# Conditioning chunks of the output stage issued by GpSimd instead of SyncE in a hybrid decoder block

## The chip, the cores and the metric

The kernel runs on one core of a Trainium2 chip. The metric is the device time of one execution in microseconds (us). The other times in this document come from profiled executions: one execution that the hardware profiler recorded, with times from the start of its span.

## What is computed

One decoder layer for two groups of requests, a prompt of 256 tokens and 8 samples of 4 tokens, which share all weights. Each layer turns a conditioning vector `c` into six vectors (shift, scale and gate, twice), mixes with a pooling mixer and a Mamba-2 mixer, projects back with `w_out`, adds the gated result, and ends with a gated feed-forward part.

```python
def block(x, c, st_pool, st_conv, st_ssm, st_ffn, pos0, lp):
    mod = silu(c) @ lp['w_ada'] + lp['b_ada']
    sh1, sc1, g1, sh2, sc2, g2 = split(mod, 6)
    h = rmsnorm(x, lp['norm1']) * (1 + sc1) + sh1
    u_pool, z, xbc, dt_raw = split(h @ lp['w_in'])
    pool_out, new_pool = pool_mixer(u_pool, st_pool, ...)
    ssd_out, new_conv, new_ssm = ssd_mixer(z, xbc, dt_raw, st_conv, st_ssm, ...)
    mix = concatenate([pool_out, ssd_out]) @ lp['w_out']
    x = x + g1 * mix
    h2 = rmsnorm(x, lp['norm2']) * (1 + sc2) + sh2
    ffn_out, new_ffn = conv_ffn(h2, st_ffn, ...)
    x = x + g2 * ffn_out
```

The width is 2048 and all values are 32-bit floats. The six vectors are called parts 0 to 5 here. Part 2 is `g1`, part 3 is `sh2`, part 4 is `sc2`, part 5 is `g2`.

## The kernel before

**Tiling.** The 2048 channels are 16 tiles of 128 partitions (`KT` = 16). The prompt's 256 columns and the samples' 32 are worked on side by side, 288 columns in a matmul. Each product in 32-bit precision is made of three matmuls for every 128x128 block of weights (`mm3`): high half of the weight by high half of the operand (L312), high by low (L313), low by high (L314). The high half of a weight chunk is a cast on ScalarE (`whi_...`, L298), the low half a subtraction on VectorE (`wlo_...`, L300).

**Weights.** All weights come from one array in chunks of at most 128x1024 floats, 512 KB. `load` takes a slot of a ring of buffers and issues the transfer (L279) on SyncE's queue (SP). Two rings matter here: `raw` for weights that are split, such as `raw_out_m_h` (half h of output block m), and `rawa` for conditioning chunks, such as `raw_adap_4_k_h` (part 4, channel tile k, half h), which are multiplied as they are (L414). In the output stage the ring `rawa` has thirteen slots in three pools: 4, and 4 and 5 that are added as room comes free.

**Conditioning.** `ada_visits` loads the chunks of a part ahead and then, in visits, multiplies them (`whole`). For part 4 a visit covers four channel tiles, so 8 chunks and 32 matmuls of 512 columns; there are four visits in the output stage, behind the blocks m=3, 6, 9 and 12.

**Output stage.** It makes 16 blocks m of `x + g1 * mix`. For each m `out_units` runs 16 channel tiles: 12 into the accumulator `mm_out`, 4 into `mm_outp`, 48 matmuls in all. VectorE then scales `mm_out` by the norm (`oz`, L1179), adds it and `mm_outp` to the prompt's columns of `x` (L1169) and makes the samples' product `rs` (L1172), which GpSimd adds to `x` (L1175). ScalarE squares the new `x` (`sqa`, L1185) and GpSimd sums the squares (`rt`, L1187 and L1189). Loads of `x` (L1213) are issued by SP. `mixl` (L1121) is the low half of the operand of this stage, made by VectorE ahead of it.

**GpSimd's other work here.** It writes the state `o_pool` (L1115), loads `stf` (the feed-forward state, L1280) and prepares `gb` buffers for the feed-forward part (a memset at L1291, a copy out of `stf` at L1292).

**What sets the order.** Each engine executes its instructions in one fixed order. The order isn't that of the source: a scheduler places every instruction, transfers included, by when it reckons its inputs and its buffer slot to be there. Instructions marked `keep_in_program_order` keep theirs. A transfer's completion is counted on one of 8 lanes for SP and ScalarE together and 8 for GpSimd, taken in turn. A transfer is issued only when the one that had the same lane before it has landed.

Of the kernel before, what the change touches and what calls it, by code (L numbers as in the profile page):

```python
# [18 lines left out]
P = 128  # L19
# [35 lines left out]
AK, AO = 2, 4  # L55
# [28 lines left out]
def _xbc_chunks(bi):  # L84
    (k0, gk), (a, b) = BLOCKS[bi]
    mper = RAWC // (gk * P)
    cuts = [a, *([4, 8] if bi == 0 else []), *range(a + (12 if bi == 0 else mper), b, mper), b]
    return [(list(range(k0, k0 + gk)), list(range(m, n))) for m, n in zip(cuts, cuts[1:])]
# [35 lines left out]
def _halves(nk):  # L124
    return [(0, 8), (8, nk - 8)]
# [41 lines left out]
def kernel(ctx: ExitStack, tc, ins, outs):  # L167
    nc = tc.nc
    S = _STREAM
    wflat = ins["wflat"]  # L170
# [102 lines left out]

    wp = [None]

    def load(key, ring="raw"):
        off, cols = S.items[key]
        t = wp[0].tile([P, RAWC], F32, tag=ring, name="raw_" + "_".join(map(str, key)))
        nc.sync.dma_start(t[:, :cols], wflat[off:off + P * cols].rearrange("(p n) -> p n", p=P))  # L279
        return t  # L280

    queue = deque(_need_order())
    ahead = {}
    nloads = [0]

    def top_up():

        while queue and nloads[0] - min((n for n, _ in ahead.values()), default=nloads[0]) < RAW0 + RAW1 + RAWA:
            key = queue.popleft()
            ahead[key] = (nloads[0], load(key))  # L290
            nloads[0] += 1
# [4 lines left out]
    def split_steps(raw, a, n, name):  # L296
        hi = wp[0].tile([P, RAWC], F32R, tag="whi", name="whi_" + name)
        yield nc.scalar.copy(hi[:, :n], raw[:, a:a + n])  # L298
        lo = wp[0].tile([P, RAWC], F32R, tag="wlo", name="wlo_" + name)
        yield hi, lo, nc.vector.tensor_tensor(lo[:, :n], raw[:, a:a + n], hi[:, :n].bitcast(F32), ALU.subtract)  # L300
# [17 lines left out]
    def project_units(key, nk, opnd=None, order=None):  # L318

        name = "_".join(map(str, key))  # L320
        ps = pm.tile([P, 512], F32, tag="mm", name="mm_" + name)
        for h, (k0, n) in enumerate(_halves(nk)):
            hi, lo = ready.pop(key + (h,), None) or split(load(key + (h,)), 0, n * P, f"{name}_{h}")
            for i in range(n):
                k = k0 + i
                ko = order[k] if order else k
                bh, bl = (xhi[0][ko], xlo[0][ko]) if opnd is None else opnd(k)
                mm3(ps[:, :N], hi, lo, i, bh, bl, k == 0, k == nk - 1)
                if k % YK == YK - 1 or k == nk - 1:
                    yield ps  # L330
# [7 lines left out]
    def ada_sb(ps, nb, name, r=P):  # L338
        asb = kp.tile([P, 512], F32, tag="asb", name="asb_" + name)
        nc.scalar.copy(asb[0:r, :nb], ps[0:r, :nb])  # L340
        return asb
# [13 lines left out]
    def ada_group_units(gi):  # L355
# [8 lines left out]
        for q0 in range(0, nq, AQ[gi]):  # L364
            raws = [(q, fetch(("ada", gi, q)) if gi else load(("ada", gi, q)))
                    for q in range(q0, min(q0 + AQ[gi], nq))]

            order = [(q, raw, kk) for q, raw in (raws[::-1] if gi else raws) for kk in range(0, per, kstep)]
            for n, (q, raw, kk) in enumerate(order):
                if gi == 0 and kk == 0:  # L370
                    yield
                k = q * per + kk
                for j in range(nj if gk > 1 else 4):
                    if gk == 1:

                        ck, c = k + j // 2, kk * 256 + j * P
                    else:
                        ck, c = k, kk * nj * nb + j * nb
                    begun = gi > 0 and n + j > 0
                    with tc.high_priority() if begun else nullcontext():  # L380
                        i = nc.tensor.matmul(ps[32 * j:32 * j + 32, :nb], sc_c[:, ck, :], raw[:, c:c + nb],  # L381
                                             start=q0 + n == 0, stop=q0 + AQ[gi] >= nq and n + 1 == len(order),
                                             tile_position=(0, 32 * j))
                    if begun:
                        tc.keep_in_program_order(i)
            if gi and q0 + AQ[gi] < nq:
                yield
# [20 lines left out]
    def whole(ps, chunks, step, pin, begun=0):  # L408

        n = 0  # L410
        for k, h, raw in chunks[::-1]:
            for j in (2 * h, 2 * h + 1):
                with tc.high_priority() if n else nullcontext():
                    i = nc.tensor.matmul(ps[32 * j:32 * j + 32, :], sc_c[:, k, :],  # L414
                                         raw[:, 512 * (j % 2):512 * (j % 2) + 512], start=not begun and k == step - 1,
                                         stop=k == KT - step, tile_position=(0, 32 * j))
                if n or pin:
                    tc.keep_in_program_order(i)
                n += 1

    def ada_visits(parts, step, ps=None, begun=0, apart=False):

        plan = [(part, k0) for part in parts for k0 in range(begun, KT, step)]
        ahead, end = [], None

        def chunks(v):
            part, k0 = plan[v]
            for k in range(k0, k0 + step):
                for h in range(2):
                    ahead.append((k, h, load(("adap", part, k, h), "rawa")))  # L430
                    if apart:
                        yield
            for _ in range(1 if apart else 3):
                yield

        yield from chunks(0)
        for v, (part, k0) in enumerate(plan):
            if end:
                ada_end(*end)
                end = None  # L440
            if k0 == 0:
                ps = pa.tile([P, 512], F32, tag="ada", name=f"adap{part}")
            whole(ps, ahead, step, True, begun)
            ahead.clear()
            if k0 + step == KT:
                end = part, ada_sb(ps, 512, f"p{part}")
            yield
            if v + 1 < len(plan):
                yield from chunks(v + 1)
        ada_end(*end)  # L450
        yield

    def ada_end(part, asb):
        pt = ada_tr(asb, 512, f"p{part}")
        with tc.high_priority():
            nc.vector.tensor_tensor(ada[:, part].rearrange("p (j i) c -> p i j c", j=4),
                                    pt.rearrange("p (i j c) -> p i j c", i=4, j=4)[:, :, :, 0:NC9],
                                    bada[:, part].rearrange("p (j i) -> p i j", j=4).unsqueeze(3)
                                    .to_broadcast([P, 4, 4, NC9]), ALU.add)
        if part == 4:  # L460
            ada_scale(1, 4, vec[:, V_N2:V_N2 + KT], 0, KT)
# [76 lines left out]
    for q in range(4):  # L538
        t = mx.tile([P, 4, N], F32, tag="blk", name=f"xa{q}", bufs=4)
# [416 lines left out]
    def chain(*gens):  # L956
        for gn in gens:
            yield from gn

    adas = ada_visits((2, 3), AK)  # L960
    with in_order(*(e.engine for e in (nc.tensor, nc.scalar, nc.vector))):
        nc.scalar.activation(warm, sc_c[:, 0, 0:1], AF.Sqrt, scale=0.0)
        warm_pe(WU[0])
        ssum = aux("ssum1")
        for q in range(4):
# [5 lines left out]
            for i in range(4):  # L971
# [18 lines left out]
        parts = [split_steps(t, 0, len(ms) * P, f"xbc0_{i}") for i, (t, (_, ms)) in  # L990
                 enumerate(zip(first, _xbc_chunks(0)))]
# [55 lines left out]
    for bi in range(len(BLOCKS)):  # L1047
        last = bi + 1 == len(BLOCKS)
        top_up()
        if last:  # L1050
# [6 lines left out]
            raw = load(("dt",))[:, :KT * NH].rearrange("p (k h) -> p k h", h=NH)  # L1057
# [6 lines left out]
            ps = pm.tile([P, 512], F32, tag="mm", name="mm_dt")  # L1064
# [26 lines left out]
    n = 0  # L1091
# [13 lines left out]
            next(late[m])  # L1105
    drain(adas)
    wp[0].move("rawa", "rawa", "raw")
    adas = ada_visits((4,), AO, apart=True)
    for h, (_, n) in enumerate(_halves(KT)):
        ready[("out", 0, h)] = split(load(("out", 0, h)), 0, n * P, f"out_0_{h}")  # L1110
    drain(back)
# [11 lines left out]
    for g in range(4):  # L1123
        for t in range(3):
            k = 4 + 3 * g + t
# [125 lines left out]
    with in_order(nc.tensor.engine, nc.scalar.engine, nc.vector.engine):  # L1251
# [8 lines left out]
        for k in (0, 0, 1, 0, 1):  # L1260
            next(mod[k], None)
        rstd2 = rstd2()
        drain(mod[1])
        ready[("upk", 2)] = upk(2)
    adag2 = ada_visits((5,), AO, ps5, GA, True)
    up0 = [(pm.tile([P, 512], F32, tag="mm", name=f"mm_up{i}") if i < 3 else aux(f"mm_up{i}"))
           for i in range(2 * FK)]
# [131 lines left out]
    with in_order(nc.sync.engine, nc.scalar.engine, nc.vector.engine):  # L1399
        for i, (m0, n, own) in enumerate(YC):  # L1400
            v = x[:, m0:m0 + n, :]
            eng, r = (nc.gpsimd, rstdf) if own else (nc.vector, rstdp)
# [148 lines left out]
```

## Time and profile before

| | us |
|---|---|
| median of 3 runs | 1345.59 (1345.21 to 1346.12) |
| the profiled execution | 1346.4 |
| its span | 1344.6 |
| output stage in it | about 361 to 488 |
| matmul of 288 columns, mean | 0.29 to 0.30, one every 0.13 |

"Span" is the time from the first to the last recorded instruction; the execution's own time lies 1.8 us above it. In rows of the timeline stand the start, the duration, the engine, the line, the operation with output and inputs, the number of instructions put together in the row, and in brackets how long the engine had been idle before and who released it. PE is TensorE, DVE VectorE, ACT ScalarE, POOL GpSimd, SP SyncE; SPq and POOL rows with DMA_DIRECT2D are the issues of transfers, and their landing comes later. A summary of one tile ends with the time from issue to landing (minimum, median, maximum). Traffic on SP's queue (q1) is 310.72 MB of the program's 323.19 MB, and on GpSimd's (q0) 9.69 MB.

### The profile page before, as it was taken

The numbers are of one execution on the slowest core, as the hardware profiler recorded it, in microseconds if no ns is written. First come the engines' busy times: TensorE is split into PE (matmuls) and PEld (weight loads), VectorE is DVE, ScalarE is ACT, GpSimd is POOL, SyncE is SP. The second block draws the span as 40 slices with busy tenths as digits, with TensorE's granted clock in tenths as the row PEclk, the third lists the DMA queues.
The fourth block names the chain that finished last, engine by engine and source line by source line (L and its number), as shares of the span: only waits on it lengthen the run. The fifth ranks groups of instructions, "written<-read, shape, count | busy, mean of one in ns | idle before, by whom it ended". The sixth has DMA issues, their size and how long they took to land.

```text
span 1344.6 us, 26157 instructions
## 1 busy us (share of the span) xinstructions
PE 1328.4 (99%) x10523; PEld 1247.1 (93%) x10523; DVE 822.8 (61%) x1375; ACT 580.3 (43%) x913; POOL 223.1 (17%) x449
## 2 busy tenths in 40 slices
PE   9999999999999999999999999999999999999997
PEld 7899988776788889999999999999999999999997
DVE  5776569878754568555565455665655556666543
ACT  5243244677733335433433333434433334443552
POOL 0000012123122222102121001221210011122221
PEclk9999999999999999999999999999999999999999
DMA  9999778888898866687455455555544555555521
GB/s 375 405 370 373 272 266 308 308 318 299 306 402 354 324 237 228 229 311 282 172 201 171 167 179 184 203 185 196 182 162 172 190 190 193 194 190 191 188 69 71
DMA packets 97482, 323.19 MB, mean 240 GB/s; under 512 B 10768, under 2 KB 19920, under 8 KB 97360
## 3 DMA queue, kind: packets, MB, share of 16 engines
q1 hardware_dynamic: 93456, 310.72, 63.0%
q0 software_dynamic: 3184, 9.69, 2.0%
q8 instruction: 82, 1.34, 0.4%
q10 hardware_dynamic: 720, 1.11, 0.2%
q14 instruction: 40, 0.33, 0.1%
HBM read 309.78 MB, written 10.39 MB: 238 GB/s over the span
## 4 chain that ended last, share of the span: by engine, by line
PE 93%; DMA 3%; DVE 2%; ACT 1%; issue 0%; POOL 0%; SPq 0%; DVEq 0%; ACTq 0%; POOLq 0%
PE mm_down L313 7%; PE mm_down L312 7%; PE mm_down L314 7%; PE mm_val L313 6%; PE mm_gate L313 6%; PE mm_gate L312 6%; PE mm_gate L314 6%; PE mm_val L314 6%; PE mm_val L312 6%; PE xbc L312 4%; PE xbc L313 4%; PE xbc L314 4%; PE adap L414 4%; PE adag L381 2%; DMA raw_adap<-wflat 2%; PE mm_out L314 2%
## 5 line engine op out<-in xcount | busy, mean ns | idle before, releaser
L313 PE MATMUL mm_down<-al,whi_down 128*128 128x288 f32 x688 | 202.5, 294 | 0.0
L312 PE MATMUL mm_down<-ah,whi_down 128*128 128x288 f32 x688 | 202.4, 294 | 0.0
L314 PE MATMUL mm_down<-ah,wlo_down 128*128 128x288 f32 x688 | 202.0, 294 | 0.0
L313 PE MATMUL mm_val<-h2l,whi_val 128*128 128x288 f32 x640 | 189.1, 296 | 0.0
L313 PE MATMUL mm_gate<-h2l,whi_gate 128*128 128x288 f32 x640 | 189.1, 295 | 0.0
L314 PE MATMUL mm_val<-h2h,wlo_val 128*128 128x288 f32 x640 | 188.4, 294 | 0.0
L314 PE MATMUL mm_gate<-h2h,wlo_gate 128*128 128x288 f32 x640 | 188.4, 294 | 0.0
L312 PE MATMUL mm_gate<-h2h,whi_gate 128*128 128x288 f32 x640 | 188.3, 294 | 0.0
L312 PE MATMUL mm_val<-h2h,whi_val 128*128 128x288 f32 x640 | 188.0, 294 | 0.0
L300 DVE TENSOR_TENSOR wlo_down<-raw_down,whi_down 128x1024 fp32r<-128x1024 f32 x96 | 109.1, 1137 | 115.4 <-ACT whi_down L298 115.4
L300 DVE TENSOR_TENSOR wlo_gate<-raw_gate,whi_gate 128x1024 fp32r<-128x1024 f32 x80 | 98.9, 1237 | 131.5 <-ACT whi_gate L298 131.5
L298 ACT CAST whi_down<-raw_down 128x1024 fp32r<-128x1024 f32 x96 | 92.3, 962 | 164.7 <-PE mm_down L313 135.3
L298 ACT CAST whi_gate<-raw_gate 128x1024 fp32r<-128x1024 f32 x80 | 84.1, 1051 | 156.6 <-PE mm_gate L313 80.3
L298 ACT CAST whi_val<-raw_val 128x1024 fp32r<-128x1024 f32 x80 | 84.1, 1052 | 129.3 <-issue 110.1
L312 PE MATMUL xbc<-h1h,whi_xbc 128*128 128x288 f32 x448 | 133.1, 300 | 0.8 <-ACT h1h L491 0.7
L313 PE MATMUL xbc<-h1l,whi_xbc 128*128 128x288 f32 x448 | 132.3, 296 | 0.0
L314 PE MATMUL xbc<-h1h,wlo_xbc 128*128 128x288 f32 x448 | 130.1, 295 | 0.0
L312 PEld LDWEIGHTS mm_down<-ah,whi_down 128*128 128x128 f32 x688 | 129.2, 188 | 0.0
L313 PEld LDWEIGHTS mm_down<-al,whi_down 128*128 128x128 f32 x688 | 129.1, 188 | 0.0
L314 PEld LDWEIGHTS mm_down<-ah,wlo_down 128*128 128x128 f32 x688 | 129.0, 188 | 0.0
L312 PEld LDWEIGHTS mm_gate<-h2h,whi_gate 128*128 128x128 f32 x640 | 120.3, 188 | 2.5 <-issue 2.5
L314 PEld LDWEIGHTS mm_gate<-h2h,wlo_gate 128*128 128x128 f32 x640 | 120.5, 188 | 0.0
(337 smaller groups left out, 2978.8 us busy)
## 6 DMA issues: line engine op xcount, KB each, us to landing
raw_adap<-wflat SPq DMA_DIRECT2D x128, 512.0 KB, 6.6
raw_gate<-wflat SPq DMA_DIRECT2D x80, 512.0 KB, 3.5
raw_val<-wflat SPq DMA_DIRECT2D x80, 512.0 KB, 3.5
raw_ada<-wflat SPq DMA_DIRECT2D x64, 512.0 KB, 9.6
raw_xbc<-wflat SPq DMA_DIRECT2D x50, 512.0 KB, 9.8
raw_down<-wflat SPq DMA_DIRECT2D x48, 512.0 KB, 3.4
raw_out<-wflat SPq DMA_DIRECT2D x32, 512.0 KB, 9.7
raw_down<-wflat SPq DMA_DIRECT2D x32, 384.0 KB, 3.5
```

Source lines behind the costliest of these rows:

```text
L298: yield nc.scalar.copy(hi[:, :n], raw[:, a:a + n])
L300: yield hi, lo, nc.vector.tensor_tensor(lo[:, :n], raw[:, a:a + n], hi[:, :n].bitcast(F32), ALU.subtract)
L312: nc.tensor.matmul(ps, whi[:, w], bh, start=first, stop=False)
L313: nc.tensor.matmul(ps, whi[:, w], bl, start=False, stop=False)
L314: nc.tensor.matmul(ps, wlo[:, w], bh, start=False, stop=last)
L381: i = nc.tensor.matmul(ps[32 * j:32 * j + 32, :nb], sc_c[:, ck, :], raw[:, c:c + nb], start=q0 + n == 0, stop=q0 + AQ[gi] >= nq and n + 1 ...
L414: i = nc.tensor.matmul(ps[32 * j:32 * j + 32, :], sc_c[:, k, :], raw[:, 512 * (j % 2):512 * (j % 2) + 512], start=not begun and k == step - 1,
```

## The change

`load` and `ada_visits` take the engine that issues, and the visits of part 4 pass GpSimd. So the 32 chunks `raw_adap_4_k_h`, 16 MB in all, go through GpSimd's instruction stream and queue. All the other loads stay on SP. Sizes, rings and slots are the same, and the scheduler places everything anew.

```diff
-    def load(key, ring="raw"):
+    def load(key, ring="raw", eng=nc.sync):
         off, cols = S.items[key]
         t = wp[0].tile([P, RAWC], F32, tag=ring, name="raw_" + "_".join(map(str, key)))
-        nc.sync.dma_start(t[:, :cols], wflat[off:off + P * cols].rearrange("(p n) -> p n", p=P))
+        eng.dma_start(t[:, :cols], wflat[off:off + P * cols].rearrange("(p n) -> p n", p=P))
         return t
...
-    def ada_visits(parts, step, ps=None, begun=0, apart=False):
+    def ada_visits(parts, step, ps=None, begun=0, apart=False, eng=nc.sync):
...
             for k in range(k0, k0 + step):
                 for h in range(2):
-                    ahead.append((k, h, load(("adap", part, k, h), "rawa")))
+                    ahead.append((k, h, load(("adap", part, k, h), "rawa", eng)))
...
     drain(adas)
     wp[0].move("rawa", "rawa", "raw")
-    adas = ada_visits((4,), AO, apart=True)
+    adas = ada_visits((4,), AO, apart=True, eng=nc.gpsimd)
```

What the scheduler makes of it is shown at three places. The first is SP at the beginning of the output stage, where block 2 and then block 3 are loaded. Before (the last number of a name only tells tiles apart):

```order
L279 DMA raw_out_2_0_4815<-wflat 128x1024
L279 DMA raw_out_2_1_4849<-wflat 128x1024
L279 DMA raw_adap_4_0_0_4757<-wflat 128x1024
L279 DMA raw_adap_4_0_1_4777<-wflat 128x1024
L279 DMA raw_adap_4_1_0_4803<-wflat 128x1024
L279 DMA raw_adap_4_1_1_4833<-wflat 128x1024
L1213 DMA x_4715<-x 128x1152 x2
L279 DMA raw_adap_4_2_0_4847<-wflat 128x1024
L279 DMA raw_adap_4_2_1_4879<-wflat 128x1024
L279 DMA raw_out_3_0_4896<-wflat 128x1024
L279 DMA raw_adap_4_3_0_4908<-wflat 128x1024
L279 DMA raw_adap_4_3_1_4928<-wflat 128x1024
```

and now:

```order
L279 DMA raw_out_2_0_4815<-wflat 128x1024
L279 DMA raw_out_2_1_4849<-wflat 128x1024
L279 DMA raw_out_5_0_5074<-wflat 128x1024
L279 DMA raw_out_5_1_5108<-wflat 128x1024
L279 DMA raw_out_6_0_5155<-wflat 128x1024
L1213 DMA x_4715<-x 128x1152 x2
L279 DMA raw_out_3_0_4896<-wflat 128x1024
L279 DMA raw_out_3_1_4930<-wflat 128x1024
L279 DMA raw_out_4_0_4992<-wflat 128x1024
```

Where the chunks of part 4 were, three halves of the blocks 5 and 6 now stand ahead of `x` and of block 3. Before, these three came after block 4.

The second is GpSimd at the same time, one piece of the difference. Its `stf` load, memsets and `gb` copies stood right behind `o_pool` before; these rows are the upper part of what stands there now:

```order
 L1115 DMA o_pool<-npl_4566 128x540
+L279 DMA raw_adap_0_0_4757<-wflat 128x1024
+L279 DMA raw_adap_0_1_4777<-wflat 128x1024
+L279 DMA raw_adap_1_0_4803<-wflat 128x1024
+L279 DMA raw_adap_1_1_4833<-wflat 128x1024
+L279 DMA raw_adap_2_0_4847<-wflat 128x1024
+L279 DMA raw_adap_2_1_4879<-wflat 128x1024
+L279 DMA raw_adap_3_0_4908<-wflat 128x1024
+L279 DMA raw_adap_3_1_4928<-wflat 128x1024
+L1175 TENSOR_TENSOR x<-x,rs_0_4721 128x32
```

Further down in the same piece:

```order
+L279 DMA raw_adap_6_0_5106<-wflat 128x1024
+L1175 TENSOR_TENSOR x<-x,rs_2_4870 128x32
 L1280 DMA stf<-st_ffn 128x688
+L1175 TENSOR_TENSOR x<-x,rs_2_4888 128x32
 L1291 MEMSET gb_6560 128x2
 L1291 MEMSET gb_6579 128x2
+L1189 TENSOR_TENSOR rt_4716<-rt_4716,sqa_4891 128x288
 L1292 COPY gb_6560<-stf 128x8x2
 L1292 COPY gb_6579<-stf 128x8x2
```

Eight chunks now follow `o_pool`, and the `stf` load and the copies that wait for it have moved behind the `x` additions of the first three blocks. The chunks 6_1, 7_0, 7_1 and 8_0 follow later, behind the square of block 3.

The third is ScalarE in the middle of the stage (`sqa_5068` is the square of block 4, `sqa_5150` of 5, `sqa_4987` of 3):

```order
-L298 CAST whi_out_0_5076<-raw_out_0_5074 128x1024
-L1185 ACTIVATE sqa_5068<-x 128x288
-L298 CAST whi_out_1_5110<-raw_out_1_5108 128x1024
 L298 CAST whi_out_0_5157<-raw_out_0_5155 128x1024
-L1185 ACTIVATE sqa_5150<-x 128x288
 L298 CAST whi_out_1_5191<-raw_out_1_5189 128x1024
 L298 CAST whi_out_0_5252<-raw_out_0_5250 128x1024
+L1185 ACTIVATE sqa_5068<-x 128x288
 L298 CAST whi_out_1_5284<-raw_out_1_5282 128x1024
```

The casts of the blocks 5, 6 and 7 stood behind the squares of the blocks 4 and 5 and now stand ahead of them.

## The prediction

> **What bounds the kernel now.** I read the page first: busy time by engine, then the chain that ended last.
>
> ```profile
> PE 1328.4 (99%) x10523; PEld 1247.1 (93%) x10523; DVE 822.8 (61%) x1375; ACT 580.3 (43%) x913; POOL 223.1 (17%) x449
> ...
> PE 93%; DMA 3%; DVE 2%; ACT 1%; issue 0%; POOL 0%; SPq 0%; DVEq 0%; ACTq 0%; POOLq 0%
> ```
>
> TensorE sets the end, and the change takes no matmul away. So there is nothing to win except the gaps in PE's stream, and nothing to lose except new ones. The output stage, where the moved chunks are loaded, runs from about 361 to 488 us. The stretches of 20 us show it next (columns: length, busy time of PE, PEld, DVE, ACT, POOL, granted clock, DMA share, GB/s):
>
> ```profile
> 377.00:397.00 20.00, 19.54 (x150) 16.30 (x148) 11.71 (x23) 6.07 (x9) 6.56 (x12) 1.00 1.03 411
> 397.00:417.00 20.00, 19.37 (x143) 18.57 (x140) 9.52 (x16) 6.66 (x8) 2.63 (x6) 1.00 1.00 400
> ```
>
> Two things stand there: PE is idle 0.46 and 0.63 us in a stretch, and the DMA engines are full for 40 us. At 411 GB/s a chunk of 512 KB (524,288 bytes) costs 1.28 us, an `x` load (128x1152 floats, 589,824 bytes) 1.43 us, and `stf` (352,256 bytes) 0.86 us. What is queued ahead of a chunk is therefore what its landing costs. PE's waits from 355 to 500 us name one releaser for nearly all of it, the low half of an output weight:
>
> ```profile
> PE mm_out L314 <- DVE wlo_out L300: 1.5, 4, 0.5
> ```
>
> These are the four waits in PE's timeline, each with the matmul before it:
>
> ```profile
> 386.42 0.29 PE L313 MATMUL mm_out<-mixl,whi_out 128*128 128x288 f32 x1
> 387.18 0.40 PE L314 MATMUL mm_out<-mixh,wlo_out 128*128 128x288 f32 x1 [0.46 <-DVE wlo_out L300]
> ...
> 407.04 0.29 PE L312 MATMUL mm_outp<-mixh,whi_out 128*128 128x288 f32 x1
> 407.51 0.40 PE L314 MATMUL mm_out<-mixh,wlo_out 128*128 128x288 f32 x1 [0.18 <-DVE wlo_out L300]
> ...
> 414.20 0.29 PE L313 MATMUL mm_outp<-mixl,whi_out 128*128 128x288 f32 x1
> 414.95 0.40 PE L314 MATMUL mm_out<-mixh,wlo_out 128*128 128x288 f32 x1 [0.45 <-DVE wlo_out L300]
> ...
> 437.84 0.29 PE L313 MATMUL mm_outp<-mixl,whi_out 128*128 128x288 f32 x1
> 438.58 0.40 PE L314 MATMUL mm_out<-mixh,wlo_out 128*128 128x288 f32 x1 [0.45 <-DVE wlo_out L300]
> ```
>
> Matmuls otherwise start 0.13 us apart. So the four cost 387.18 − 386.42 − 0.13 = 0.63, then 0.34, 0.62 and 0.61 us. They have two causes. The last three are a matter of order on ScalarE: the cast stood behind a `sqa` that waited for GpSimd's `x`.
>
> ```profile
> 404.82 0.44 ACT L1185 ACTIVATE sqa<-x 128x288 f32<-128x288 f32 x1 [6.46 <-POOL x L1175]
> 405.17 1.98 ACT L298 CAST whi_out<-raw_out 128x1024 fp32r<-128x1024 f32 x2
> ...
> 412.25 0.45 ACT L1185 ACTIVATE sqa<-x 128x288 f32<-128x288 f32 x1 [5.10 <-POOL x L1175]
> ```
>
> The first one, at 387.18, is a matter of DMA. It belongs to weight half (3,0), the first half of output block m=3. Its load, cast and subtraction follow each other (SP's row with the time from issue to landing, then ACT, then DVE):
>
> ```profile
> L279 SPq DMA_DIRECT2D raw_out<-wflat x1: 328/328/328, 373.8 to 373.8; - x1
> ...
> DMA to landing us min/median/max: 10.5/10.5/10.5
> ```
> ```profile
> 384.39 1.05 ACT L298 CAST whi_out<-raw_out 128x1024 fp32r<-128x1024 f32 x1 [1.47 <-DMA raw_out<-wflat]
> ```
> ```profile
> 385.90 1.22 DVE L300 TENSOR_TENSOR wlo_out<-raw_out,whi_out 128x1024 fp32r<-128x1024 f32 x1
> ```
>
> Issued at 373.78, landed 10.5 us later at 384.28, cast, subtracted by 387.12, used at 387.18. There is no slack: one more microsecond in front of this transfer is one more microsecond for the program.
>
> **What now stands ahead of (3,0).** SP's timeline of that time, and what held (3,0) on SP, the `mixl` on DVE whose end at 373.76 frees its place:
>
> ```profile
> 367.49 1.75 SPq L279 DMA_DIRECT2D raw_adap<-wflat  x4
> 369.29 1.11 SPq L1213 DMA_DIRECT2D x<-x  x2
> 370.72 1.06 SPq L279 DMA_DIRECT2D raw_adap<-wflat  x2
> 373.78 0.33 SPq L279 DMA_DIRECT2D raw_out<-wflat  x1
> 374.16 2.49 SPq L279 DMA_DIRECT2D raw_adap<-wflat  x2
> 377.65 1.71 SPq L279 DMA_DIRECT2D raw_out<-wflat  x2
> ```
> ```profile
> 370.02 2.35 DVE L300 TENSOR_TENSOR wlo_out<-raw_out,whi_out 128x1024 fp32r<-128x1024 f32 x2
> ...
> 373.30 0.46 DVE L1121 TENSOR_TENSOR mixl<-pout,mixh 128x288 fp32r<-128x288 f32 x1 [0.42 <-ACT mixh L1120]
> ```
>
> Before, six conditioning chunks and two `x` loads are issued ahead of (3,0), and two more chunks only after it. In the changed program three things are different. GpSimd issues eight chunks back to back, from 367.5 on (the first SP row: the last visit of part 3 has to be through). SP, with nothing of its own left to do, issues (5,0), (5,1) and (6,0) before `x` and (3,0): they wait only for the splits of (1,0), (2,0) and (2,1), which end about 367.9, 371.2 and 372.4 (the DVE row at 370.02 holds the last two). And the `stf` load of 0.86 us is no longer in that crowd, since GpSimd now issues it much later. (3,0) still waits for `mixl` and is issued at 373.8.
>
> GpSimd's own issue rows:
>
> ```profile
> 365.22 0.56 POOL L1115 DMA_DIRECT2D o_pool<-npl  x1 [0.30 <-POOL npl L1114]
> 365.78 0.55 POOL L1280 DMA_DIRECT2D stf<-st_ffn  x1
> ...
> 370.67 1.75 POOL L1292 COPY gb<-stf 128x16 f32<-128x16 f32 x2 [4.20 <-DMA stf<-st_ffn]
> ```
>
> An issue costs 0.56 us there against 0.33 on SP. Eight from 367.5 are out by about 372, before (3,0) is issued. All 32 cost 32 × 0.56 = 18 us of GpSimd, which lies in its idle time (6.56 busy of 20 in the fullest stretch); without that cover it would delay L1175, `sqa` and the casts behind it. SP's relief, 32 × 0.33 us, is worth nothing, as nobody waits for an issue of SP.
>
> If transfers are served in about the order of issue, (3,0) has 2 more chunks and 3 output halves ahead of it and `stf` less: 5 × 1.28 − 0.86 = 5.5 us. It lands at 384.28 + 5.5 = 389.8, is cast by 390.95 and subtracted by 392.2, and PE goes on at 392.25 instead of 387.18: **+5.1 us**. The residual hides in that. `x` lands one transfer before (3,0), and the DVE work on it took 3 us after it came:
>
> ```profile
> 379.04 0.48 DVE L1169 SCALAR_TENSOR_TENSOR x<-oz,ada,x 128x256 f32<-128x256 f32 x1 [0.57 <-DMA x<-x]
> ...
> 381.87 0.18 DVE L1172 TENSOR_TENSOR rs<-mm_outp,ada 128x32 f32<-128x32 f32 x1
> ```
>
> **What is won.** On ScalarE the casts now stand further ahead of the squares: (5,1), (6,1) and (9,1), the three that were late, no longer follow the squares of blocks 4, 5 and 8. Their waits go: −(0.34 + 0.62 + 0.61) = **−1.6 us**. At most that, at least nothing: the squares they now follow belong to earlier blocks.
>
> Moved matmuls on PE (the four `mm_outp` rows per block) keep their number and cost nothing: the same stream in another order, behind the same visits. Loads of the next stage move on SP after 450 us, where DMA has room, and cost nothing.
>
> The sum: +5.1 − 1.6 = +3.5 us on the profiled execution's 1346.4, so 1349.9. The runs' median 1345.59 lies 0.8 below that execution: **1349.1**.
>
> **How do two queues share?** The whole question is in "about the order of issue". The nearest row is a small GpSimd write under a backlog of SP chunks:
>
> ```profile
> L743 POOL DMA_DIRECT2D o_conv<-ncv x1: 557/557/557, 210.8 to 210.8; - x1
> ...
> DMA to landing us min/median/max: 6.7/6.7/6.7
> ```
> ```profile
> L279 SPq DMA_DIRECT2D raw_adap<-wflat x1: 423/423/423, 209.3 to 209.3; - x1
> L279 SPq DMA_DIRECT2D raw_xbc<-wflat x1: 617/617/617, 209.8 to 209.8; - x1
> ...
> DMA to landing us min/median/max: 10.5/10.9/11.3
> ```
>
> It was issued at 210.75 and landed at 217.45, 6.7 us later and some 2 to 4 us before two chunks that were issued 1.4 and 0.9 us ahead of it (209.34 + 10.5 and 209.81 + 11.3). So its own queue gives it some right of way, but far from all: it waited for most of the backlog. This is nearest to order of issue, which I take; equal turns and full right of way are the other bounds.
>
> [...]
>
> **The rivals.** *Equal turns.* SP's queue holds (5,0), (5,1), (6,0), two `x` and (3,0): 4 × 1.28 + 2 × 1.43 = 8.0 us of transfer. GpSimd's eight chunks are 10.2. With equal shares only 8.0 of these are served by the time (3,0) is, so it lands 2.2 us before the first case, at 387.6, and PE resumes at 390.05: +2.9 − 1.6 = +1.3, **1346.9**. For it: `o_conv` overtook. Against it: 6.7 us for one small transfer.
>
> *The other side: chunks on a queue of their own don't hold up SP's.* Then (3,0) waits only for the 8.0 us of its own queue, lands by 373.8 + 8.0 = 381.8, its low half is ready by 384.1, before m=3 begins at 386.29 (one matmul ahead of the quoted 386.42), and the first wait goes too: −1.6 − 0.6 = −2.2, **1343.4**. It decides once (3,0) lands before 383.7: L314 would be due at 386.55, and from landing to L314 the first case above took 387.18 − 384.28 = 2.9 us. For it: six chunks no longer stand on SP ahead of (3,0). Against it: the 411 GB/s are shared, and `o_conv` was no faster.
>
> *GpSimd is held in order.* Its `gb` copies wait for `stf`. Before, that cost nothing at 370.67 (the row above). Now `stf` is issued after GpSimd's add of the square of m=1, which stands on ScalarE behind the cast of (3,0): about 393. Queued behind the copies are the `x` of m=3, its square, the casts of (6,0) to (7,0) behind that, and chunks 6_1 to 8_0, due in the second visit:
>
> ```profile
> 417.80 0.64 PE L414 MATMUL adap<-raw_adap,sc_c 128*32 128x512 f32 x4
> ```
>
> With landings of 10.5 us, as (3,0) had, `stf` is there at 403.5, the copies are done at 405.3, and 6_1 to 7_1 are issued by about 409 and land by 419.5. The visit would begin at 417.8 + 3.5 = 421.3, so 2 us remain. If both landings take 2.5 us longer, the visit waits about 3 us: **1352**. For it: DMA is full here. Against it: by then SP has fewer transfers outstanding.
>
> **How the numbers follow.** Order of issue 0.50 (1349.1, its own range 1347.5 to 1351), equal turns 0.20 (1346.9), GpSimd held 0.15 (1352), no hold-up 0.15 (1343.4). The range from 1345 to 1353 leaves out the last and the top of the third. A measurement of this kernel tells about 0.2%, 2.7 us, from no change, so the bounds are 1342.9 and 1348.3. Slower: 0.40 of the first, 0.06 of the second, all of the third, 0.61. Same: 0.10, 0.14 and 0.04 of the last, 0.28. Faster: 0.11.
>
> **What would show it.** Right: in the new trace (3,0) is issued about 373.8 and lands near 390, one PE wait of about 5 us stands in front of the first L314 of m=3, and the waits of blocks 5, 6 and 9 are gone. Equal turns: the same wait, some 3 us long. No hold-up: the wait gone, (3,0) landed by 382. GpSimd held: a wait of PE before the visit near 421, released by `raw_adap`, and POOL idle before L1292 until past 406. The prediction is wrong in its ground if the longest PE wait of the stage stands anywhere else, or if a landing before 384 goes with no gain.

## The result, and the profile after

| | before | changed |
|---|---|---|
| median of 6 runs, us | 1345.80 (1345.21 to 1346.21) | 1350.93 (1349.86 to 1353.22) |
| the profiled execution's span, us | 1344.6 | 1348.9 |

The changed kernel is slower: ratio 1.0040, with a 95% interval from 1.0028 to 1.0053. The forecast was 1349.1 us with a range from 1345 to 1353.

Busy time and the chain, from the page of the changed kernel:

```profile
PE 1330.0 (99%) x10523; PEld 1249.4 (93%) x10523; DVE 821.8 (61%) x1375; ACT 581.8 (43%) x913; POOL 241.5 (18%) x481
...
PE 90%; DMA 6%; DVE 1%; issue 1%; POOL 0%; ACT 0%; SPq 0%; DVEq 0%; POOLq 0%; ACTq 0%
```

DMA's share of the chain has doubled from 3% to 6%. GpSimd is busy 241.5 − 223.1 = 18.4 us longer, about the 32 × 0.56 = 18 us of issues that the prediction had; they lie in its idle time. The stretches of the output stage (columns as before: length, busy PE, PEld, DVE, ACT, POOL, granted clock, DMA share, GB/s):

```profile
377.00:397.00 20.00, 15.52 (x97) 14.67 (x97) 8.46 (x16) 4.25 (x6) 5.78 (x11) 0.83 1.03 410
397.00:417.00 20.00, 20.00 (x157) 17.20 (x156) 12.77 (x24) 7.83 (x10) 11.76 (x23) 1.00 1.02 407
417.00:437.00 20.00, 19.29 (x151) 16.42 (x150) 9.37 (x17) 5.71 (x8) 7.63 (x15) 1.00 1.03 409
```

The loss stands in one stretch: from 377 to 397 us PE is busy 15.52 us instead of 19.54, and its granted clock is 0.83 instead of 1.00. The DMA engines are full as before, and now until 437. PE's waits from 355 to 500 us (in total, times, longest):

```profile
PE mm_out L312 <- ACT whi_out L298: 4.1, 1, 4.1
PE adap L414 <- DMA raw_adap<-wflat: 0.7, 1, 0.7
PE mm_out L314 <- DVE wlo_out L300: 0.4, 1, 0.4
```

The four short waits on `wlo_out` have become one long wait, a short one right behind it, and a wait of the second visit on its chunks. PE's timeline at the long wait, which is the start of block 3:

```profile
386.28 0.29 PE L314 MATMUL mm_outp<-mixh,wlo_out 128*128 128x288 f32 x1
390.64 0.61 PE L312 MATMUL mm_out<-mixh,whi_out 128*128 128x288 f32 x1 [4.07 <-ACT whi_out L298]
391.05 0.44 PE L313 MATMUL mm_out<-mixl,whi_out 128*128 128x288 f32 x1
391.90 0.61 PE L314 MATMUL mm_out<-mixh,wlo_out 128*128 128x288 f32 x1 [0.41 <-DVE wlo_out L300]
392.31 0.44 PE L312 MATMUL mm_out<-mixh,whi_out 128*128 128x288 f32 x1
392.55 0.44 PE L313 MATMUL mm_out<-mixl,whi_out 128*128 128x288 f32 x1
...
395.83 0.30 PE L312 MATMUL mm_out<-mixh,whi_out 128*128 128x288 f32 x1
395.96 0.30 PE L313 MATMUL mm_out<-mixl,whi_out 128*128 128x288 f32 x1
```

The first L314 of block 3 starts at 391.90, against 387.18 before. After it the matmuls stand 0.24 us apart, not 0.13, until 395.8. The stretches of 2 us say why (the clock is the third number from the end):

```profile
387.00:389.00 2.00, 0.00 (x0) 0.00 (x0) 0.00 (x0) 0.00 (x0) 1.34 (x4) 0.97 1.04 414
389.00:391.00 2.00, 0.35 (x1) 0.36 (x2) 0.38 (x1) 1.39 (x2) 0.00 (x0) 0.50 1.02 408
393.00:395.00 2.00, 2.00 (x10) 2.00 (x10) 1.23 (x1) 0.51 (x2) 0.57 (x2) 0.50 1.03 412
```

The granted clock fell to one half during the wait, at 388.9, and stayed there until 395.7. The load of (3,0) behind all that, from SP's queue:

```profile
L279 SPq DMA_DIRECT2D raw_out<-wflat x1: 367/367/367, 374.8 to 374.8; - x1
...
DMA to landing us min/median/max: 14.6/14.6/14.6
```

It landed at 374.82 + 14.6 = 389.4 us. And GpSimd's first eight chunks:

```profile
L279 POOL DMA_DIRECT2D raw_adap<-wflat x8: 540/540/551, 367.8 to 371.8; - x8
...
DMA to landing us min/median/max: 4.7/11.3/18.6
```

They were issued within 4 us, but the first landed at 372.5 and the last at 390.4: seven intervals in 17.9 us, 2.56 us each on average. That is twice the 1.28 us that one chunk costs. SP's transfers landed in between, the halves (5,1) and (6,0) at 378.9 and 381.5, then the two `x` loads:

```profile
L1213 SPq DMA_DIRECT2D x<-x x2: 434/919/1404, 372.8 to 373.3; - x2
...
DMA to landing us min/median/max: 11.4/12.5/13.6
```

These landed at 384.2 and 386.9, and (3,0) followed at 389.4. So about half of the transfer rate went to GpSimd's queue and half to SP's: from 375 to 403 us q0 moved 5.60 MB and q1 5.87 MB, 410 GB/s in all. In the kernel before q1 alone moved 11.47 MB in that time.

Where the time is, by the starts of PE's instructions in both profiled executions (us):

| | before | changed | difference |
|---|---|---|---|
| last matmul of block 2 | 386.16 | 386.28 | +0.12 |
| first L314 of block 3 | 387.18 | 391.90 | +4.72 |
| last matmul of block 3 | 393.36 | 399.66 | +6.30 |
| last matmul of block 6 | 417.57 | 422.48 | +4.91 |
| second visit | 417.80 | 423.48 | +5.68 |
| last matmul of block 9 | 441.20 | 446.07 | +4.87 |
| last matmul of block 15 | 487.94 | 492.81 | +4.87 |

So: +4.7 for the late (3,0), +1.6 for the half clock, −1.4 for the waits of blocks 5 and 6 that are gone, +0.8 for the second visit, −0.8 for the wait of block 9 that is gone.

### The profile page after: what moved, and what is told of

Its sections match the earlier page's. It is cut to its first block, busy times and chain, and to the rows that moved or that the text cites. A ratio compares the mean times of both kernels' runs of the same rounds, so it can differ in the third digit from the quotient of the medians.

```text
span 1348.9 us, 26177 instructions
## 1 busy us (share of the span) xinstructions
PE 1330.0 (99%) x10523; PEld 1249.4 (93%) x10523; DVE 821.8 (61%) x1375; ACT 581.8 (43%) x913; POOL 241.5 (18%) x481
## 4 chain that ended last, share of the span: by engine, by line
PE 90%; DMA 6%; DVE 1%; issue 1%; POOL 0%; ACT 0%; SPq 0%; DVEq 0%; POOLq 0%; ACTq 0%
PE mm_down L313 7%; PE mm_down L312 7%; PE mm_down L314 7%; PE mm_val L313 6%; PE mm_gate L313 6%; PE mm_gate L312 6%; PE mm_gate L314 6%; PE mm_val L314 6%; PE mm_val L312 6%; PE xbc L312 4%; PE xbc L313 4%; PE xbc L314 4%; PE adap L414 3%; DMA raw_adap<-wflat 3%; PE adag L381 2%; DMA raw_out<-wflat 2%
## 5 line engine op out<-in xcount | busy, mean ns | idle before, releaser
L314 PE MATMUL mm_down<-ah,wlo_down 128*128 128x288 f32 x688 | 202.0, 294 | 0.0
L314 PE MATMUL mm_val<-h2h,wlo_val 128*128 128x288 f32 x640 | 188.4, 294 | 0.0
L314 PE MATMUL mm_gate<-h2h,wlo_gate 128*128 128x288 f32 x640 | 188.4, 294 | 0.0
L314 PE MATMUL xbc<-h1h,wlo_xbc 128*128 128x288 f32 x448 | 130.1, 295 | 0.0
L314 PEld LDWEIGHTS mm_down<-ah,wlo_down 128*128 128x128 f32 x688 | 129.0, 187 | 0.0
L314 PEld LDWEIGHTS mm_gate<-h2h,wlo_gate 128*128 128x128 f32 x640 | 120.5, 188 | 0.0
```

Source lines behind the costliest of these rows:

```text
L314: nc.tensor.matmul(ps, wlo[:, w], bh, start=False, stop=last)
```

## The experiments

All ratios are to the kernel before, with 95% intervals. In the diffs `add_manual_dep(a, b, ...)` makes the scheduler issue `a` behind `b` on their engine, without a wait for `b` to finish (`AFTER` names that kind of dependence).

**1. SP's output halves in the order of the blocks, chunks still on GpSimd.** This undoes the part of the change that the scheduler made on SP, except that it now issues the two `x` loads earlier than in either kernel, at 363.9 and 364.4. So (3,0) has less of its own queue ahead of it.

```diff
-        eng.dma_start(t[:, :cols], ...)
+        in_turn(key, eng.dma_start(t[:, :cols], ...))
...
+    def in_turn(key, i): key[0] == "out" and (last_out and tc.add_manual_dep(i.ins, last_out[-1], AFTER), last_out.append(i.ins.name))
```

> The changed kernel with one thing different: SP issues the output halves in the order of the blocks, so (5,0), (5,1) and (6,0) stand behind (4,1) again; the conditioning chunks stay on GpSimd. Theory 1 (the loss is the place of (3,0) on SP, and the two queues take turns chunk by chunk): only two x loads and, in turns with them, GpSimd chunks are ahead; (3,0) is issued at 373.8, lands near 378 to 380, the 4 us wait and the slow matmuls after it go, and the three waits of blocks 5, 6 and 9 stay away: 1343.4 to 1345, if the second visit doesn't wait longer than its 0.7 us; up to 1348 if it does. Theory 2 (transfers are served in order of issue over both queues): eight chunks are still ahead of it, it lands at 384.3 + 2 x 1.28 - 0.86 = 386.0, PE waits some 2 us: 1346 to 1347. Theory 3 (a second queue as such costs the time): (3,0) lands after 388 and the time stays at 1350 to 1351.

Measured: 1352.26 us, ratio 1.0044 (1.0032 to 1.0056). No theory had this time. (3,0), then the two chunks that GpSimd issued at 368.6 and 369.1:

```profile
L279 SPq DMA_DIRECT2D raw_out<-wflat x1: 327/327/327, 372.8 to 372.8; - x1
...
DMA to landing us min/median/max: 7.4/7.4/7.4
```
```profile
L279 POOL DMA_DIRECT2D raw_adap<-wflat x2: 540/540/540, 368.6 to 369.1; - x2
...
DMA to landing us min/median/max: 11.2/12.2/13.2
```

(3,0) landed at 380.2, as theory 1 said, and overtook a chunk that had been issued 3.6 us before it and landed at 382.3. So order of issue over both queues is refuted; that the two queues shared the rate about equally in the changed kernel is what the landings above show. The wait ahead of block 3 is gone. What came instead is a wait of the second visit (first row: PE's waits; second: GpSimd's timeline; third: the stretch of the visit):

```profile
PE adap L414 <- DMA raw_adap<-wflat: 6.1, 1, 6.1
```
```profile
404.70 0.33 POOL L1292 COPY gb<-stf 128x16 f32<-128x16 f32 x2 [7.77 <-DMA stf<-st_ffn]
```
```profile
417.00:437.00 20.00, 14.89 (x95) 9.77 (x96) 7.39 (x14) 4.22 (x5) 6.78 (x14) 0.83 1.02 403
```

GpSimd stood 7.77 us at its `gb` copies until `stf` had landed, and only after that could issue the last chunks that the second visit needs. That is the third rival of the prediction. It was hidden in the changed kernel, since there PE came to the visit 5 us later; the 0.7 us wait was its edge.

**2. The same, and `stf` issued among the first chunks.** Until now it stood behind the thirteenth chunk (the expectation says the twelfth).

```diff
     x = ff.tile([P, KT, N], F32, name="x")
+    stf = ff.tile([P, FT, NB, 2], F32, name="stf")
+    with tc.high_priority():
+        nc.gpsimd.dma_start(stf, ins["st_ffn"])
...
-    stf = ff.tile([P, FT, NB, 2], F32, name="stf")
-    nc.gpsimd.dma_start(stf, ins["st_ffn"])
```

> The kernel with SP's output halves in the order of the blocks, and in addition the stf load issued by GpSimd among its first chunks instead of after the twelfth. If GpSimd's wait for stf ahead of its gb copies is what makes the chunks of the second visit late, that visit no longer waits and the time lies 0.5 to 2 us below the kernel with the order alone; if those chunks are late because the DMA engines are full, the two are equal within 0.5 us.

Measured: 1346.23 us, ratio 0.9998 (0.9989 to 1.0007), 6.0 us less than with the order alone. The visit's wait shrank but did not go:

```profile
PE adap L414 <- DMA raw_adap<-wflat: 2.2, 1, 2.2
```

The expected gain was too small: `stf` held back 4 us of wait and the half clock that came with it (0.83 from 417 to 437 us there; 1.00 in every 2 us from 413 to 425 us here).

What is left of the wait is again a matter of order. In every kernel here with chunks on GpSimd, the scheduler issues 8_1 and 9_0 ahead of 6_1, 7_0 and 7_1, which the list under the change does not show. The third visit needs the first two, the second visit the other three. Here are those two in this kernel, and then 7_1, with PE's wait for it:

```profile
L279 POOL DMA_DIRECT2D raw_adap<-wflat x2: 577/577/577, 398.3 to 399.3; - x2
...
DMA to landing us min/median/max: 9.5/10.3/11.0
```
```profile
L279 POOL DMA_DIRECT2D raw_adap<-wflat x1: 537/537/537, 402.5 to 402.5; - x1
...
  PE adap L414: 2.2, 1
...
DMA to landing us min/median/max: 15.7/15.7/15.7
```

8_1 and 9_0 landed at 407.8 and 410.3, and 7_1 at 418.1, just before PE went on at 418.19. Two places earlier, at 2.56 us each, 7_1 would have been there at 413.0, before PE was through with block 6 (this is an estimate from the 2.56 us a chunk of the changed kernel; no run takes the two out of the way). So with two defects mended and this one left, the chunks on GpSimd give nothing over the kernel before. What they would give without it stays open.

**3. The first visit's eight chunks on SP, the other 24 on GpSimd.**

```diff
-                    ahead.append((k, h, load(("adap", part, k, h), "rawa", eng)))
+                    ahead.append((k, h, load(("adap", part, k, h), "rawa", eng if v else nc.sync)))
```

> The changed kernel with the eight chunks of the first visit issued by SP as before, and the other 24 by GpSimd. SP's order up to (4,0) is then that of before. Theory 1 (the place of (3,0) behind five other transfers): (3,0) lands at 384 to 385, its wait is at most 0.5 us, the waits of blocks 5, 6 and 9 are gone: 1343.5 to 1345. Theory 3 (GpSimd issuing or a second queue costs the time wherever it is): 1348 or more.

Measured: 1350.43 us, ratio 1.0030 (1.0019 to 1.0041). A miss for theory 1 as I had applied it. (3,0) and the chunks that GpSimd issued by then:

```profile
L279 SPq DMA_DIRECT2D raw_out<-wflat x1: 328/328/328, 373.4 to 373.4; - x1
...
DMA to landing us min/median/max: 14.6/14.6/14.6
```
```profile
L279 POOL DMA_DIRECT2D raw_adap<-wflat x3: 540/545/548, 369.6 to 370.6; - x3
...
DMA to landing us min/median/max: 8.0/10.1/12.3
```

(3,0) landed at 388.0, not at 384.3. GpSimd had room in the ring for three more chunks, and they landed among SP's transfers, the first at 377.6 and the third at 382.9, so 2.65 us apart: 3 × 1.28 = 3.8 us, about the difference of 3.7 us to the kernel before. I had counted SP's queue only.

**4. The same, with GpSimd's chunks held until it has worked on block 0.**

```diff
-        (nc.vector if m == KT - 1 else nc.gpsimd).tensor_tensor(xs, xs, t, ALU.add)
+        x_done.append((nc.vector if m == KT - 1 else nc.gpsimd).tensor_tensor(xs, xs, t, ALU.add).ins.name)
...
+        i = eng.dma_start(t[:, :cols], ...); eng is nc.gpsimd and tc.add_manual_dep(i.ins, x_done[0], ...)
```

> The kernel with the first visit's eight chunks on SP, where in addition GpSimd issues no chunk before it has added the samples of block 0 (about 379), so that its three early chunks can't take turns ahead of (3,0). If these three chunks are what put the landing of (3,0) from 384.3 to 388.0 in the kernel without the hold (3 x 1.28 = 3.8 us), it lands at 384 to 385 again and PE waits at most 0.6 us there; with the waits of blocks 5, 6 and 9 gone the time is 1344 to 1345, if the second visit's chunks come in time, and up to 1347 if they don't. If something else on GpSimd's side delays (3,0), it lands near 388 again and the time stays at 1350.

Measured: 1348.64 us, ratio 1.0014 (1.0005 to 1.0023). (3,0) first, then (3,1), the second half of block 3, then PE's longest wait:

```profile
L279 SPq DMA_DIRECT2D raw_out<-wflat x1: 328/328/328, 373.9 to 373.9; - x1
...
DMA to landing us min/median/max: 10.2/10.2/10.2
```
```profile
L279 SPq DMA_DIRECT2D raw_out<-wflat x1: 327/327/327, 377.4 to 377.4; - x1
...
DMA to landing us min/median/max: 14.3/14.3/14.3
```
```profile
PE mm_out L312 <- ACT whi_out L298: 2.5, 1, 2.5
```

(3,0) landed at 384.1: the three chunks were the cause. (The hold also moved the `stf` load back ahead of the chunks, issued at 365.1 instead of 386.1; that could only make (3,0) later.) But as soon as GpSimd issued again, at 379.7, the next half had its chunks beside it, the first of which landed at 386.8, and landed itself at 391.8, against 388.1 in the kernel before. The wait moved on by half a block. In these two kernels one half of block 3 is late either way; which one it is depends on when GpSimd starts.

**5. `stf` early, nothing else** (the diff of 2 alone).

> The changed kernel with one thing different: the stf load is issued by GpSimd among its first chunks instead of after the twelfth, so its gb copies don't hold up the chunks of the second visit. The wait of 4 us ahead of block 3 and the slow matmuls behind it stay, and the second visit's wait of 0.7 us goes: about 1350.2. If stf has no part in that visit's wait, nothing changes: 1350.9.

Measured: 1349.95 us, ratio 1.0026 (1.0016 to 1.0036). PE waits for no chunk any more in this stage; the wait ahead of block 3 is there (4.7 us). Within the intervals the time itself can't be told from the changed kernel's.

**6. Idle matmuls in TensorE's stall.** Three kernels: 28 of them in the changed kernel, 28 and then 20 with `stf` early.

```diff
         pp = aux(f"mm_outp_{m}")
+        if m == 3:
+            for _ in range(28):
+                tc.keep_in_program_order(nc.tensor.matmul(pz[:, :P], ones, ones, start=True, stop=True))
```

> The changed kernel with 28 idle matmuls (128x128 of ones, about 3.1 us) for TensorE in its stall ahead of block 3, into an accumulator that block 3 starts anew. If the 16 matmuls that stood 0.24 us apart after the stall were slow because the granted clock fell in it, they stand 0.13 us apart now, (3,0) lands at 389.4 as before, and the time falls by 16 x 0.11 = 1.7 us to about 1349.2. If they were slow for another reason (full DMA engines, late operands), the time stays at 1350.9 or rises.

Measured: 1350.47 us, ratio 1.0032 (1.0021 to 1.0043). The stretch of the stall, the idle matmuls in PE's timeline, and the wait of the second visit:

```profile
377.00:397.00 20.00, 20.00 (x162) 19.96 (x161) 8.03 (x17) 4.98 (x6) 6.57 (x13) 1.00 1.03 410
```
```profile
385.12 6.41 PE L1134 MATMUL mm_out<-ones 128*128 128x128 f32 x56
```
```profile
PE adap L414 <- DMA raw_adap<-wflat: 2.3, 1, 2.3
```

The clock stayed at 1.00 and block 3 ran with 0.13 us between its matmuls. But each idle matmul was recorded as two, the 28 took 6.4 us instead of about 3.1 and ended 0.8 us after the low half of (3,0) was there, and the second visit then waited 2.3 us instead of 0.7.

> The kernel with the early stf load, and the 28 idle matmuls in TensorE's stall ahead of block 3. With the idle matmuls alone the second visit's chunks came 2.3 us late and took the gain back. With both, neither is in the way: block 3 runs at the full clock, the visit doesn't wait, and the time is 1.7 us below that of the kernel with the early stf load alone, about 1348.5. If the price of the low clock was not real, the two are equal.

Measured: 1349.14 us, ratio 1.0020 (1.0012 to 1.0029), 0.8 us under the kernel of 5 and not beyond the intervals.

> The kernel with the early stf load and idle matmuls in TensorE's stall ahead of block 3, 20 of them instead of 28. The 28 took 6.4 us and ended 0.8 us after block 3's first low half was there, which ate part of what they gave; 20 take 20/28 of that, 4.6 us, and end before it. If the low clock after the stall costs 1.5 to 1.8 us, block 3 starts as without them and then runs at the full clock: 1349.95 - 1.6 = 1348.3. If the clock's price is only the 0.8 us by which the kernel with 28 was faster, the time is 1349.1 or more.

Measured: 1349.40 us, ratio 1.0024 (1.0015 to 1.0033): the time did not fall. The profile says both why, and that the clock's price is real. From the last matmul of block 2 to the last of block 3 it is 13.84 us without idle matmuls (385.26 to 399.10) and 12.29 with the 20 (385.62 to 397.91): 1.55 us less, with the wait for (3,0) unchanged. The granted clock was 1.00 from 377 to 397 us with the 20, and 0.50 from 389 to 393 without. And the visit took it back:

```profile
PE adap L414 <- DMA raw_adap<-wflat: 2.0, 1, 2.0
```

In five kernels with the changed kernel's order on SP (it and the four of 5 and 6) the second visit began between 422.1 and 423.5 us, whatever PE did before it. In all but that of 5 its last chunk, 7_1, landed within 0.1 us before; in that of 5 it landed 0.9 us before. So there are two gates one behind the other, the landing of (3,0) and the landing of 7_1, behind 8_1 and 9_0 here too, and they cost about the same. Taking one away gives next to nothing.

**7. The kernel before, with squares behind casts on ScalarE.** The only gain that the prediction saw in the change, without the change.

```diff
-            cast, (hi, lo, rest) = split_steps(raw, a, n, name)
+            cast, (hi, lo, rest) = split_steps(raw, a, n, name); last_cast[:] = [cast.ins.name]
...
-            nc.scalar.activation(sq[:, c], x[:, m, c], AF.Square)
+            i = nc.scalar.activation(sq[:, c], x[:, m, c], AF.Square); m < KT - 1 and tc.add_manual_dep(i.ins, last_cast[0], ...)
...
+                if i == 4:
+                    squares(m - 1, "a")
...
-        squares(m, "a")
+        if m == KT - 1: squares(m, "a")
```

> The kernel before, with all chunks on SP and one thing different on ScalarE: the square of a block is issued behind the cast of the next block's second half. If the three waits of blocks 5, 6 and 9 came from casts that stood behind a square, as the prediction had it, they go and the wait at 387.18 stays: 1345.8 - 1.6 = 1344.2. If those casts would have been late anyway (landing, buffers), the time stays at 1345.8.

Measured: 1343.57 us, ratio 0.9978 (0.9968 to 0.9988). PE's waits from 355 to 500 us are one row:

```profile
PE mm_out L314 <- DVE wlo_out L300: 0.5, 1, 0.5
```

The three waits are gone, and this is the kernel that beats both.

**8. In addition (3,0) two chunks earlier on SP.**

```diff
+        i = nc.sync.dma_start(t[:, :cols], ...).ins; loads[key] = i; key == ("out", 3, 0) and tc.add_manual_dep(loads[("adap", 4, 2, 0)], i.name, ...)
```

> The kernel with all chunks on SP and the squares behind the casts, where in addition SP issues (3,0) two chunks earlier, ahead of the chunks 2_0 and 2_1. If one chunk more or less ahead of (3,0) is worth 1.28 us of its landing on one queue, it lands at 384.3 - 2 x 1.28 = 381.7, the last wait of the stage (0.46 us, 0.6 us with what lies around it) goes, and the time is 0.6 us below that of the kernel with the squares alone: about 1343.0. If the two chunks are then late for the first visit or for block 3's second half, a wait shows there and the time stays at 1343.6 or rises.

Measured: 1344.36 us, ratio 0.9984 (0.9975 to 0.9993), no gain over 7. (3,0), then PE's waits, then a stretch of 2 us behind them:

```profile
L279 SPq DMA_DIRECT2D raw_out<-wflat x1: 328/328/328, 372.6 to 372.6; - x1
...
DMA to landing us min/median/max: 9.4/9.4/9.4
```
```profile
PE mm_out L312 <- ACT whi_out L298: 1.2, 1, 1.2
...
PE mm_out L314 <- DVE wlo_out L300: 0.5, 1, 0.5
```
```profile
391.00:393.00 2.00, 2.00 (x9) 2.00 (x10) 1.51 (x1) 0.72 (x1) 0.43 (x1) 0.50 1.02 411
```

It landed at 372.57 + 9.4 = 382.0, where 381.7 was expected: two chunks fewer ahead of it on one queue made it 2.3 us earlier, near the 2 × 1.28 that was reckoned. But PE, no longer held at (3,0), came earlier to (3,1), which landed no earlier (at 388.4), and waited there.

## Where the prediction was right, and where not

**That the late (3,0) sets the loss: right.** It was forecast to land at 389.8 and PE to go on at 392.25; it landed at 389.4 and PE went on at 391.90. The term of +5.1 measured +4.7.

**"Transfers are served in about the order of issue": wrong**, though the number came out. What the runs show is nearest to the rival called equal turns: a chunk every 2.56 us in the changed kernel, with SP's transfers in between, 5.60 MB on one queue and 5.87 on the other from 375 to 403 us, and a transfer that overtakes one issued 3.6 us before it in experiment 1. In turns, seven of GpSimd's eight chunks were ahead of (3,0), and only the last, issued 3 us earlier (371.8 against 374.8), landed after it, at 390.4. Against the kernel before, one chunk and three halves more were ahead of (3,0): 384.3 + 4 × 1.28 = 389.4, where it landed. The prediction had counted the eighth chunk too (+1.28) and had taken off `stf` (−0.86). That saving did not come: the engines moved 284 GB/s from 365 to 373 us, against 322 before, so the room that `stf` left stayed empty. The two errors nearly cancel, and that the landing came out within 0.4 us is luck.

The rival's own sum of 387.6 was too early for two reasons. It counted 8.0 us of GpSimd's transfers (6.3 chunks) and not seven chunks (9.0), as if both queues had begun to fill at once, while GpSimd's first chunks were served when SP had little to send (from 367.5 to 375 us q0 moved 1.76 MB and q1 0.70). And it took the same 0.86 off for `stf`. I gave more weight to one small write (`o_conv`, 6.7 us from issue to landing) than it could carry.

**The three waits of blocks 5, 6 and 9: right in kind, low in size.** They went, and gave 1.4 + 0.8 = 2.2 us in the changed kernel instead of 1.6. Experiment 7 gained 2.2 us of span (1344.6 to 1342.4) and 2.8 us on the medians of its own comparison (1346.34 to 1343.57) by the same means, without moving a chunk, where 1.6 was expected. The sum had counted only the gap to the matmul that waited. It left out the spacing of 0.24 us right after each, three times 0.11, and a delay of 0.2 us at 410.8 that is too short for the list of waits.

**The clock: missing from the sum.** A wait of 4 us was priced at its own length. The half clock behind it cost another 1.6 us, which the 20 idle matmuls confirm inside block 3 (1.55 us).

**GpSimd held in order: a rival at 0.15, and present.** It cost 0.8 us in the changed kernel, where the other loss covers it, and 6.15 us of wait as soon as that was mended. The copies were through at 405.5, as that rival had it, but 7_1 landed at 423.4 and not by 419.5: 8_1 and 9_0 went ahead of it, and from 407.9 to 423.4 us SP's queue moved 3.15 MB beside the 3.14 of GpSimd's.

The sum was +3.5 and the profiled spans differ by +4.3 (stage alone +4.9): −0.4 for the first wait, +1.6 for the clock, −0.6 for the three waits, +0.8 for the visit. The medians differ by 5.1; the changed kernel's runs scatter over 3.4 us, the kernel before's over 1.0. That DMA had room after 450 us was wrong: its share in the kernel before was 1.02 from 450 to 460 us and 0.99 from 460 to 480. Still nothing was lost there, since the difference is +4.87 us at block 9 as at block 15.

**The rival on the other side**, that chunks on a queue of their own would not hold up SP's stream, fell: (3,0) landed 5 us later than before, and half of the full rate (5.60 of 11.47 MB from 375 to 403 us) went to the other queue.

## What to carry to other kernels

In the kernel before one queue kept the DMA engines full (share 1.00 to 1.03 from 377 to 417 us), and its order was the program's list of what is needed first; a second queue took half of the rate (a chunk every 2.56 us instead of 1.28) for whatever stood in it, due or not. Before a stream is moved to another engine, look for the first transfer without slack, count what both queues hold when it is issued, and look at what the new engine waits for ahead of its later issues, and in which order it issues them. When one gate is taken away, expect the next one close behind: here the order of casts and squares on ScalarE was worth more than any place of the chunks that was tried.

## What the runs showed of the hardware that was not expected

The granted clock fell to 0.50 during or within 1.1 us after PE's waits of 4.07, 4.70, 3.11, 6.15 and 2.53 us (the changed kernel and experiments 5, 3, 1 and 4) and stayed at 1.00 after 2.24 and 2.33 us (experiment 2, and experiment 6 with 28 idle matmuls in the changed kernel). The length of a wait alone does not decide: in experiment 8 the clock fell at 391.0 after waits of only 1.17 and 0.47 us.

How long it stayed at 0.50 differed too: 6.83 us in the changed kernel (388.87 to 395.70), 6.8 us in experiments 1, 3 and 5, and 3.4 us in experiments 4 and 8 (these five worked out from the mean clock of the stretches around). What sets the moment of the fall, and of the rise, these runs do not show.
